# First projections in rounds of 2, 4, 4, 4, 2 row chunks, the first norm's sum of squares on TensorE, the first round modulated chunk by chunk

## The chip, the cores and the metric

One core of a Trainium2 chip runs the whole block; the other cores are idle. The metric is the device time of one execution in microseconds. Before the change it is 1664.97 us, the median of three runs (1662.68, 1664.97 and 1665.35).

## What is computed

One transformer block on 256 tokens of 2048 channels, in float32. The part that the change touches is the beginning, up to the first projection:

```python
mod = einsum('bd,de->be', silu(c), w_ada) + b_ada       # 12288 columns: six vectors of 2048
sh1, sc1, gt1, sh2, sc2, gt2 = split(mod, 6)
h = rms_norm(x, norm1_g) * (1 + sc1) + sh1              # x * rsqrt(mean(x*x) + 1e-6) * g
proj = einsum('btd,dc->btc', h, w_in)                   # [256, 2048] x [2048, 10064]
...
x = x + gt1 * (mixed @ w_out)
h = rms_norm(x, norm2_g) * (1 + sc2) + sh2
x = x + gt2 * (square(relu(h @ w_up)) @ w_down)
```

Between proj and mixed stand a linear recurrence over the tokens with a decay (rwkv, 16 heads of 64) and an attention with compressed, selected and window keys (nsa, 16 heads), joined by gates that are columns of proj as well.

## The kernel before, in words

**Layout.** Activations are kept transposed: a chunk is 128 channels on the partitions by 256 tokens, and 16 chunks make the 2048 channels. A projection multiplies weight tiles (two chunks, that is 256 rows of the weight matrix, by 512 columns, 0.5 MB; the tile of the first group has 352 columns) with h. Every float32 operand is split into two float32r parts, hi and lo, and each product is three matmuls: hi with hi, hi with lo, lo with hi (`mm3`, line 101). A weight tile goes through `weights` (line 217): a load by SP into one of four `raw` buffers, the hi part by ScalarE (`split`, line 189), the lo part by VectorE (line 191), each into one of three buffers. A tile of four column blocks gives 2 x 4 x 3 = 24 matmuls of 128 x 128 by 256 columns, the tile of the first group 18.

**Modulation columns.** The vector mod is made 128 columns at a time on VectorE: a dot of a [128, 2048] tile of w_ada transposed (1 MB) with silu(c), which stands on all partitions (`ada_long`, line 165, `ada_dot`, line 156). `modc[:, e]` is column block e; h of chunk j wants blocks j (shift) and 16 + j (scale), so two dots a chunk and 32 for all. The four tiles of the first round have a buffer each; all later ones take turns in two (`SLOTS = 2`, lines 163 to 171). From the rounds' end on, the other 64 column blocks come by half tiles through the `raw` buffers (`ada`, line 173).

**Norm 1** (lines 280 to 309). ScalarE squares two chunks at a time, VectorE adds the eight squares up in `sqs`, and two float32 matmuls with ones sum them over the channels into `pss`. `rs` is 1 / sqrt of it (`rsqrt`, line 297): logarithm and exponential on ScalarE and four small VectorE instructions.

**The start in rounds** (lines 182 and 379 to 396). The first projections have nine groups of columns: the small one (three tiles of up to 128 columns, to `pl`), keys of rwkv (two groups, to `prk`), values (two, which stay in PSUM, `pvp`), receptance (two, `prk`) and nsa queries (two, `pq`). Since h is not complete at first, they go by rounds over the rows:

```python
rounds = [(0, 2), (2, 2), (4, 4), (8, 4), (12, 4)]      # first chunk, number of chunks
```

A round with n chunks makes `am` (one small VectorE instruction for all n) and the n chunks of h (`modulate`, line 321, and `affine`, line 314: VectorE makes `hf`, ScalarE `hhi`, VectorE `hlo`), and then passes over all nine groups with the n/2 weight tiles of each. At the end of a group in a round its PSUM banks are copied out by ScalarE (first round) or added to what is there by VectorE (later rounds), 14 banks in a round (`acc_evac`, line 349). While a round goes on, the dots that the next one wants are spread over its weight tiles, by `pace` (line 388): as many dots for each tile as makes them all due one tile before the round's end. In the last round the two groups of queries are not run at once but put into `queue`.

**What sets the order.** The program is written in one order, and a planner with its own costs orders each engine's instructions at compile time: by priority, and among those that are ready by its reckoning. The start has the first priority, then the stream of weights and modulation (`prio(STREAM)`), then the rest. On the chip every engine goes through its own fixed order, and SP, which issues the loads, does too: an instruction that waits holds up those behind it on its engine.

**After the start.** The recurrence and the attention are chains of small instructions; between them `fill(n)` (line 264) takes steps of the projections in `queue`, half a weight tile each (12 matmuls): the queries of the last round, keys, values and merge gates, later the output projections of the branches. What is left of the queue is run at line 1067. Then come w_out, norm 2, up and down, all by the same weight stream.

Of the kernel before, what the change touches and what calls it, by code (L numbers as in the profile page):

```python
# [17 lines left out]
T = 256  # L18
# [6 lines left out]
# columns of the packed per-channel parameters  # L25
P_BADA, P_N1, P_N2, P_MU, P_A0, P_KK, P_KA, P_RK, P_LNW, P_LNB = 0, 96, 112, 128, 155, 163, 171, 179, 187, 195
P_QG, P_KG0, P_KG1, P_KG2, P_PEK, P_PEV, NPRM = 203, 204, 205, 206, 207, 223, 239
# columns of the packed constants
# [4 lines left out]
def block_kernel(ctx, tc, a):  # L33
# [116 lines left out]
    hold = []       # what the stream's next vector instructions have to stay behind  # L150
# [14 lines left out]
    def ada_long(e):  # L165
        """The same as ada, by one long load."""
        n = apn[0] if apn[0] < 4 else apn[0] % SLOTS
        r = apb[n // 2][:, n % 2]
        apn[0] += 1
        nc.sync.dma_start(r, a["w_ada_t"][e * 128:(e + 1) * 128])  # L170
        ada_dot(r, sb, prm[:, P_BADA + e:P_BADA + e + 1], modc[:, e:e + 1])

    def ada(e):
        """modc[:, e] = b_ada + w_ada[:, e*128:(e+1)*128]^T silu(c)"""
        part = sm.tile([128, 1], FT, name="adap", tag="sm1")
        for h in range(2):
            r = RAW("ar", [128, 1024])
            nc.sync.dma_start(r, a["w_ada_t"][e * 128:(e + 1) * 128, h * 1024:(h + 1) * 1024])
            ada_dot(r, sb[:, h * 1024:(h + 1) * 1024], part if h else prm[:, P_BADA + e:P_BADA + e + 1],
                    modc[:, e:e + 1] if h else part)  # L180

    rounds = [(0, 2), (2, 2), (4, 4), (8, 4), (12, 4)]
# [10 lines left out]
    # ones of head blocks and of chunk suffixes  # L193
# [6 lines left out]
    def head_sums(ps, jp, x):  # L200
        """Rows 32 jp and 32 jp + 1 of ps: the sums over the channels of the two heads of a tile of x."""
        mm(ps[32 * jp:32 * jp + 32], cs[:, C_HS:C_HS + 32], x)

    def spread(ps, jp, r):
        """These rows of r, given in two parts, on the 64 channels of either head."""
        for k in range(2):
            mm(ps, sel[32 * jp:32 * jp + 2], r[k][32 * jp:32 * jp + 2], k == 0, k == 1)
# [9 lines left out]
    def weights(segs, W):  # L217
        """segs: (source [256 rows, w], column, w); the two parts of [128, 2, W]."""
        with prio(STREAM):
            r = RAW("wr", [128, 2, W])  # L220
            for src, c0, w in segs:
                lastw[0] = nc.sync.dma_start(r[:, :, c0:c0 + w], src.rearrange("(k p) c -> p k c", p=128)).ins
            hi = whip.tile([128, 2, W], FR, name="whi", tag="whi")
            lo = wlop.tile([128, 2, W], FR, name="wlo", tag="wlo")
            split(r, hi, lo)
        return hi, lo

    starting = [True]
    later = []      # modulation columns still to come,
    pace = [0, 0]   # so many for each weight tile, and what has added up  # L230
# [8 lines left out]
    def proj(segs_of, W, ms, rhi, rlo, kps, evac, banks=None, first=True, last=True):  # L239
        """Transposed projection: out[m] [128, 256] = w[:, m]^T h over the chunk pairs kps; a generator  # L240
        that stops after every half of a pair; the last pair goes by banks."""
        nb = (len(ms) + 1) // 2
        ps = banks or [PM("pp") for _ in range(nb)]
        for i, kp in enumerate(kps):
            hi, lo = weights(segs_of(kp), W)
            next_ada(ada_long if starting[0] else ada)
            todo = [[(k, m) for m in range(len(ms))] for k in range(2)]
            if 0 and i == len(kps) - 1 and nb == 2:
                todo = [[(k, m) for k in range(2) for m in range(len(ms)) if m // 2 == b] for b in range(2)]
            for part in todo:  # L250
                for k, m in part:
                    (c0, cw), kc = ms[m], 2 * kp + k
                    o = ps[m // 2][0:cw, (m % 2) * 256:(m % 2) * 256 + 256]
                    mm3(o, hi[:, k, c0:c0 + cw], lo[:, k, c0:c0 + cw], rhi[:, kc], rlo[:, kc],
                        first and i == 0 and k == 0 and m % 2 == 0, last and i == len(kps) - 1 and k == 1)
                yield
        if evac:
            with prio(STREAM):
                for b in range(nb):
                    evac(b, ps[b])  # L260
# [3 lines left out]
    def fill(n=1):  # L264
        """The next n steps of the projections that nothing waits for yet."""
# [14 lines left out]
    pss = PX("pss", (128, 256))  # L280
    sqs = T2("sqs", [128, 2, T])
    act(sqs, xn[:, 0:2], AF.Square)
    for i in range(1, 8):
        sq = T2("sq", [128, 2, T])
        act(sq, xn[:, 2 * i:2 * i + 2], AF.Square)
        tt(sqs, sqs, sq, OP.add)
    for k in range(2):
        mm(pss, ones, sqs[:, k], k == 0, k == 1)

    def log_exp(behind):  # L290
        """The table set with both functions, behind these instructions."""
# [5 lines left out]
    def rsqrt(out, x, scale, ep, tmp):  # L297
        """out = 1 / sqrt(x * scale + ep): by logarithm and exponential, then one Newton step."""
# [15 lines left out]
    def affine(t, x, scale, r, shift, hi, lo, last=[None]):  # L314
        """The two parts of x * scale * r + shift."""
# [5 lines left out]
    def modulate(j0, n, src):  # L321
        """h chunks j0..j0+n from the normed ones."""
        last = [None]
        for j in range(j0, j0 + n, 2):
            hf = T2("hf", [128, 2, T])
            for i in range(2):
# [34 lines left out]
    # (columns, width, tiles, destination of a bank; None: stays in PSUM)  # L361
# [17 lines left out]
    for r, (j0, n) in enumerate(rounds):  # L379
        first, last = r == 0, r == len(rounds) - 1  # L380
        with prio(START + (1 << 18)):
            stt(am[:, j0:j0 + n], modc[:, 16 + j0:16 + j0 + n], 1.0, prm[:, P_N1 + j0:P_N1 + j0 + n], OP.add, OP.mult)
            lasth = modulate(j0, n, xn)
# [60 lines left out]
    def shift_mix(p, col, rows=slice(0, 128)):  # L444
        """p + (shifted p - p) mu for one channel tile [rows, 256]."""
# [5 lines left out]
    # lora inputs  # L451
# [18 lines left out]
    # the branches' gates of nsa  # L470
# [8 lines left out]
    # 1 + tanh(z / 2) in token rows; its suffix sums over chunks of 32 tokens give the decays  # L479
# [37 lines left out]
    # k: normed keys, learning rates  # L517
# [58 lines left out]
    # rows (chunk parity, b | k, token), columns a | r tokens  # L576
# [15 lines left out]
    # inverses of (I - L): one 32 x 32 system per head and chunk, by columns  # L592
# [34 lines left out]
    # token rows of v, b, k  # L627
# [11 lines left out]
    # what enters u without a state: (a k^T) v  # L639
# [27 lines left out]
    # ---- nsa: queries. They are kept in reverse order inside blocks of 128 tokens, so that the  # L667
    # bias of query p and key s depends on p + s -------------------------------------------
# [128 lines left out]
    # keys normed and on both halves of the partitions; [token, (selected | window), d] values  # L797
# [83 lines left out]
    # ---- nsa: compressed keys and values  # L881
# [46 lines left out]
    # rows (four head pairs, head, block), columns (half of the pairs, head, channel)  # L928
# [94 lines left out]
    # y_b, added with its gate; its first half keeps up with the heads  # L1023
# [41 lines left out]
    # ---- y_b, the rest  # L1065
# [61 lines left out]
    # the residual and gt2 by tokens  # L1127
# [69 lines left out]
def _pack(inp):  # L1197
    """Layout only: what the kernel reads, under the names that it reads it by."""
# [45 lines left out]
```

## Time and profile before

| | |
|---|---|
| median of three runs | 1664.97 us (1662.68 to 1665.35) |
| profiled execution, first to last instruction | 1663.5 us |
| TensorE busy | 1595.8 us, 96% |
| TensorE weight loads busy | 1459.8 us, 88% |
| VectorE busy | 1132.9 us, 68% |
| ScalarE busy | 754.1 us, 45% |
| bytes moved | 382 MB, mean 230 GB/s |

The page gives the span of the profiled execution and no time of its own around it; the three timed runs lie from 0.8 us below to 1.9 us above that span. Matmuls overlap in their pipeline, so that the duration of one (0.28 us) is more than the distance to the next (0.12 us). The share of an engine is a mean over stages with different limits; the start, which the change touches, is the first 243 us. A releaser named in a row is the instruction whose signal came last, which need not be the one that was slow.

### The profile page before, as it was taken

What the parts mean: (1) busy time and instruction counts of PE and PEld (TensorE: products, weight loads), DVE (VectorE), ACT (ScalarE), POOL (GpSimd) and SP (SyncE); (2) the same over time, 40 slices, a digit from 0 to 9 for tenths busy, and PEclk for the clock granted to TensorE, in tenths of its full rate; (3) what the DMA queues carried; (4) which work ended last, traced back from release to release, by engine and by line L of the source; (5) the groups of instructions that cost most, each with busy time, mean ns of one, the idle gap of its engine ahead of it and who ended that gap; (6) DMA issues with size and microseconds to landing.
All of it is one profiled execution on the core that took longest, in us unless ns stands there. A gap on an engine that the chain in (4) does not pass through costs nothing.

```text
span 1663.5 us, 30084 instructions
## 1 busy us (share of the span) xinstructions
PE 1595.8 (96%) x12310; PEld 1459.8 (88%) x12310; DVE 1132.9 (68%) x1632; ACT 754.1 (45%) x1079; POOL 35.6 (2%) x60
## 2 busy tenths in 40 slices
PE   5969999999999999999999899999999999999998
PEld 3968998889899889777999899999999888888886
DVE  7999876977778667777866766665654555555555
ACT  4423458527323275655534544444444444444442
POOL 0000000000000000000000000000000000000001
PEclk9989999997999999999999999999999999999999
DMA  9999767674878677654787477777776655665664
GB/s 364 318 333 346 241 192 233 207 219 153 276 220 273 224 260 264 230 169 156 266 286 258 153 239 246 247 235 252 237 203 182 204 196 190 195 196 190 193 193 147
DMA packets 171197, 382.11 MB, mean 230 GB/s; under 512 B 29281, under 2 KB 43921, under 8 KB 166706
## 3 DMA queue, kind: packets, MB, share of 16 engines
q1 hardware_dynamic: 149344, 355.79, 65.3%
q0 software_dynamic: 4192, 14.17, 2.4%
q10 hardware_dynamic: 17523, 10.24, 2.1%
q8 instruction: 96, 1.57, 0.4%
q14 instruction: 42, 0.34, 0.1%
HBM read 370.13 MB, written 10.01 MB: 229 GB/s over the span
## 4 chain that ended last, share of the span: by engine, by line
PE 76%; DVE 10%; DMA 8%; ACT 3%; issue 3%; ACTq 0%; DVEq 0%; SPq 0%
PE pp L99 45%; PE da L99 10%; PE db L99 10%; DVE wlo L90 3%; DMA ar<-in_w_ada_t 2%; DMA wr<-in_w_out 2%; PE pvp L99 2%; DVE ap L158 2%; PE y L99 1%; ACT whi L189 1%; PE po L99 1%; PE zps L99 1%; PE ups L99 1%; DMA kx<-skv 1%; DMA wr<-in_w_up 1%
## 5 line engine op out<-in xcount | busy, mean ns | idle before, releaser
L189 ACT CAST whi<-wr 128x1024 fp32r<-128x1024 f32 (+1 forms) x352 | 366.6, 1042 | 509.1 <-PE pp L99 305.6
L90 DVE TENSOR_TENSOR wlo<-wr,whi 128x1024 fp32r<-128x1024 f32 (+1 forms) x352 | 426.0, 1214 | 215.9 <-ACT whi L189 215.0
L99 PE MATMUL pp<-hhi,whi 128*128 128x256 f32 (+1 forms) x1072 | 309.8, 292 | 21.8 <-ACT hhi L87 20.8
L99 PE MATMUL pp<-hhi,wlo 128*128 128x256 f32 (+1 forms) x1072 | 302.2, 290 | 6.2 <-DVE wlo L90 6.2
L99 PE MATMUL pp<-hlo,whi 128*128 128x256 f32 (+1 forms) x1072 | 307.3, 289 | 0.2 <-DVE hlo L93 0.2
L99 PE MATMUL pp<-h2h,wlo 128*128 128x256 f32 x1024 | 289.0, 283 | 0.5 <-DVE wlo L90 0.5
L99 PE MATMUL pp<-h2l,whi 128*128 128x256 f32 x1024 | 289.0, 283 | 0.2 <-DVE h2l L93 0.2
L99 PE MATMUL pp<-h2h,whi 128*128 128x256 f32 x1024 | 287.2, 283 | 1.0 <-ACT h2h L87 1.0
L90 DVE TENSOR_TENSOR wdl<-wd,wdh 128x1024 fp32r<-128x1024 f32 x128 | 156.7, 1225 | 170.3 <-ACT wdh L189 170.0
L99 PEld LDWEIGHTS pp<-hhi,whi 128*128 128x128 f32 (+1 forms) x1072 | 209.2, 196 | 30.7 <-ACT hhi L87 22.1
L189 ACT CAST wdh<-wd 128x1024 fp32r<-128x1024 f32 x128 | 134.9, 1055 | 195.8 <-PE db L99 192.1
L99 PEld LDWEIGHTS pp<-hhi,wlo 128*128 128x128 f32 (+1 forms) x1072 | 206.1, 196 | 13.0 <-DVE wlo L90 8.5
L99 PEld LDWEIGHTS pp<-hlo,whi 128*128 128x128 f32 (+1 forms) x1072 | 209.9, 196 | 3.9 <-issue 2.7
L99 PEld LDWEIGHTS pp<-h2h,wlo 128*128 128x128 f32 x1024 | 196.4, 192 | 0.8 <-DVE wlo L90 0.7
L99 PEld LDWEIGHTS pp<-h2l,whi 128*128 128x128 f32 x1024 | 196.5, 192 | 0.6 <-DVE h2l L93 0.6
L99 PEld LDWEIGHTS pp<-h2h,whi 128*128 128x128 f32 x1024 | 195.4, 192 | 1.3 <-ACT h2h L87 1.3
L158 DVE CUSTOM_DVE_ANT_0 ar<-ar,sb,prm 128x1024 f32<-128x1024 f32 x64 | 82.0, 1281 | 53.8 <-DMA ar<-in_w_ada_t 53.8
L158 DVE CUSTOM_DVE_ANT_0 ar<-ar,sb,adap 128x1024 f32<-128x1024 f32 x64 | 81.9, 1280 | 15.4 <-DMA ar<-in_w_ada_t 15.0
L99 PE MATMUL da<-wdh,uh 128*128 128x512 f32 x256 | 78.9, 389 | 1.0 <-ACT uh L189 1.0
L99 PE MATMUL db<-wdl,uh 128*128 128x512 f32 x256 | 79.5, 389 | 0.0
L99 PE MATMUL db<-wdh,uh 128*128 128x512 f32 x256 | 79.2, 389 | 0.0
L99 PE MATMUL da<-wdh,ul 128*128 128x512 f32 x256 | 79.1, 389 | 0.0
(331 smaller groups left out, 2566.4 us busy)
## 6 DMA issues: line engine op xcount, KB each, us to landing
wr<-in_w_in SPq DMA_DIRECT2D x136, 512.0 KB, 5.0
ar<-in_w_ada_t SPq DMA_DIRECT2D x128, 512.0 KB, 4.4
wr<-in_w_up SPq DMA_DIRECT2D x128, 512.0 KB, 4.2
wd<-in_w_down SPq DMA_DIRECT2D x128, 512.0 KB, 4.3
ap<-in_w_ada_t SPq DMA_DIRECT2D x32, 1024.0 KB, 6.7
wr<-in_w_out SPq DMA_DIRECT2D x32, 512.0 KB, 5.5
wr<-in_w_in SPq DMA_DIRECT2D x40, 256.0 KB, 3.5
wr<-in_w_o_rwkv SPq DMA_DIRECT2D x16, 512.0 KB, 4.8
```

The lines of the kernel that those rows point to most:

```text
L90: return V.tensor_tensor(out, x, y, op=op).ins
L99: PE.matmul(out, l, r, start=start, stop=stop, skip_group_check=True)
L158: V.tensor_tensor_reduce(out=r, in0=r, in1=s, scale=0.5, scalar=start, op0=OP.mult, op1=OP.add, accum_out=out)
L189: S.copy(hi, raw)
```

## The change

Three edits, in code that otherwise stays as it is (the diff also takes out comments and docstrings, which is left out here). The rounds have 2, 4, 4, 4 and 2 chunks in place of 2, 2, 4, 4 and 4. The squares of norm 1 are not added up on VectorE: every one goes to TensorE, whose matmuls with ones add all 16 halves up in the PSUM bank. In the first round `am` is made for one chunk at a time, each directly before that chunk is modulated, into an `hf` tile of its own.

```diff
-    rounds = [(0, 2), (2, 2), (4, 4), (8, 4), (12, 4)]
+    rounds = [(0, 2), (2, 4), (6, 4), (10, 4), (14, 2)]
...
     pss = PX("pss", (128, 256))
-    sqs = T2("sqs", [128, 2, T])
-    act(sqs, xn[:, 0:2], AF.Square)
-    for i in range(1, 8):
+    for i in range(8):
         sq = T2("sq", [128, 2, T])
         act(sq, xn[:, 2 * i:2 * i + 2], AF.Square)
-        tt(sqs, sqs, sq, OP.add)
-    for k in range(2):
-        mm(pss, ones, sqs[:, k], k == 0, k == 1)
+        for k in range(2):
+            mm(pss, ones, sq[:, k], i == 0 and k == 0, i == 7 and k == 1)
...
         for j in range(j0, j0 + n, 2):
             hf = T2("hf", [128, 2, T])
-            for i in range(2):
+            for i in range(min(2, n)):
                 affine(hf[:, i], src[:, j + i], am[:, j + i:j + i + 1], rs, modc[:, j + i:j + i + 1], hhi[:, j + i], hlo[:, j + i], last)
...
         with prio(START + (1 << 18)):
-            stt(am[:, j0:j0 + n], modc[:, 16 + j0:16 + j0 + n], 1.0, prm[:, P_N1 + j0:P_N1 + j0 + n], OP.add, OP.mult)
-            lasth = modulate(j0, n, xn)
+            step = 1 if first else n
+            for j in range(j0, j0 + n, step):
+                stt(am[:, j:j + step], modc[:, 16 + j:16 + j + step], 1.0, prm[:, P_N1 + j:P_N1 + j + step], OP.add, OP.mult)
+                lasth = modulate(j, step, xn)
```

## Rows read from the trace of the kernel before

**Rows 1.** The page: its first line, and the busy time, share of the span and instructions of TensorE and VectorE.

```profile
span 1663.5 us, 30084 instructions
PE 1595.8 (96%) x12310; PEld 1459.8 (88%) x12310; DVE 1132.9 (68%) x1632; ACT 754.1 (45%) x1079; POOL 35.6 (2%) x60
```

**Rows 2.** Busy time of the engines in stretches: the five rounds, then the rest in three pieces. Columns: stretch, its length, busy us (and instructions) of each engine, granted TensorE clock, DMA share, GB/s.

```profile
28.40:56.60 28.20, 27.95 (x211) 27.66 (x212) 23.27 (x26) 15.38 (x25) 0.00 (x0) 1.00 0.93 336
56.60:94.70 38.10, 25.74 (x212) 25.23 (x210) 36.80 (x43) 10.99 (x14) 0.00 (x0) 0.88 0.95 324
94.70:148.00 53.30, 50.98 (x400) 50.08 (x400) 50.91 (x60) 20.25 (x25) 0.00 (x0) 0.96 0.94 344
148.00:204.00 56.00, 53.34 (x442) 53.09 (x443) 49.58 (x59) 19.94 (x23) 0.00 (x0) 1.00 0.82 276
204.00:243.00 39.00, 39.00 (x327) 38.83 (x325) 28.65 (x40) 22.48 (x32) 0.00 (x0) 1.00 0.63 182
243.00:800.00 557.00, 545.98 (x5102) 481.79 (x5101) 415.99 (x823) 283.67 (x540) 20.20 (x38) 0.96 0.69 222
800.00:950.00 150.00, 139.81 (x1124) 136.71 (x1123) 111.95 (x155) 67.41 (x83) 8.37 (x13) 0.99 0.72 241
950.00:1660.00 710.00, 703.74 (x4493) 642.78 (x4492) 393.95 (x394) 299.99 (x323) 6.79 (x6) 1.00 0.66 209
```

**Rows 3.** What TensorE waited for between 20 and 100 us (first line) and between 100 and 205 us (the others): us in total, times, the longest.

```profile
PE pp L99 <- ACT hhi L87: 20.8, 2, 11.7
...
PE pp L99 <- DVE wlo L90: 3.7, 3, 2.2
PE pvp L99 <- ACT whi L189: 1.0, 1, 1.0
```

**Rows 4.** TensorE's matmuls in order of time: the first of the projections, the last of round 1, the first of round 2. Columns: start us, us, what, with the idle time before it and who ended that.

```profile
28.48 1.22 PE L99 MATMUL pp<-hhi,whi 128*128 128x256 f32 x4 [9.15 <-ACT hhi L87]
...
82.82 0.28 PE L99 MATMUL pp<-hhi,wlo 128*128 128x256 f32 x1
94.77 1.22 PE L99 MATMUL pp<-hhi,whi 128*128 128x256 f32 x4 [11.67 <-ACT hhi L87]
```

**Rows 5.** VectorE in order of time: hlo of round 0, the first dot behind it, the first dot for round 2, the end of the eighth, am and hf of round 2. Columns as in rows 4.

```profile
29.34 0.87 DVE L93 SCALAR_TENSOR_TENSOR hlo<-hf,modc,hhi 128x256 fp32r<-128x256 f32 x2
30.13 2.34 DVE L158 CUSTOM_DVE_ANT_0 ap<-ap,sb,prm 128x2048 f32<-128x2048 f32 x1
...
53.86 2.35 DVE L158 CUSTOM_DVE_ANT_0 ap<-ap,sb,prm 128x2048 f32<-128x2048 f32 x1
...
93.38 0.08 DVE L158 DVE_READ_ACCUMULATOR2_ANT modc<- 128x1 f32 x1
93.49 0.16 DVE L93 SCALAR_TENSOR_TENSOR am<-modc,prm 128x4 f32<-128x4 f32 x1
93.69 1.67 DVE L93 SCALAR_TENSOR_TENSOR hf<-xn,am,rs 128x256 f32<-128x256 f32 x4
```

**Rows 6.** Pieces of the chain that ended last: start us, us, what. The first matmuls of round 2, a long run of matmuls in round 3 and 4, and the first work of the recurrence on TensorE.

```profile
94.77 15.21 PE pp L99 x108
...
181.45 38.36 PE pp L99 x320
...
242.84 0.25 PE gnp L475 x2
```

**Rows 7.** The granted clock in a stretch of the wait before round 2: stretch, length, TensorE busy, clock, DMA share, GB/s.

```profile
86.00:88.00 2.00, 0.00 (x0) 0.50 0.73 219
```

**Rows 8.** The loads: the first 20 us of the rows by stretch (columns as in rows 2), the next 8 us (columns as in rows 7), and the time from issue to landing of the modulation tiles between 28 and 100 us.

```profile
0.00:20.00 20.00, 9.24 (x12) 3.66 (x12) 13.43 (x27) 10.27 (x17) 0.20 (x4) 1.00 0.92 349
...
20.00:28.00 8.00, 0.00 (x0) 1.00 1.07 415
...
DMA to landing us min/median/max: 4.9/6.3/7.1
```

**Rows 9.** VectorE's groups of instructions: the splits in round 0 (28.4 to 56.6 us), and the adds of partial sums in round 1 (56.6 to 94.7 us). Columns: what xcount, busy us, mean ns, idle time before and what ended it.

```profile
L90 DVE TENSOR_TENSOR wlo<-wr,whi 128x1024 fp32r<-128x1024 f32 (+1 forms) x9 | 10.6, 1185 | 4.9 <-ACT whi L189 4.9
...
L90 DVE TENSOR_TENSOR prk<-prk,pp 128x512 f32<-128x512 f32 x8 | 5.3, 679 | 0.0
L90 DVE TENSOR_TENSOR pq<-pq,pp 128x512 f32<-128x512 f32 x4 | 2.6, 682 | 0.0
L90 DVE TENSOR_TENSOR pl<-pl,pp 128x512 f32<-128x512 f32 (+1 forms) x2 | 1.1, 549 | 1.2 <-PE pp L99 1.2
```

**Rows 10.** The first 22 us in order of time: TensorE's start matmuls (cps) with two of their weight loads, the last add of the squares on VectorE, the sum over the channels on TensorE, and the first of rsqrt's VectorE instructions.

```profile
2.74 7.16 PE L99 MATMUL cps<-crow,one 1*128 1x512 f32 x8 [2.74 <-DMA crow<-in_c]
...
4.58 0.33 PEld L99 LDWEIGHTS cps<-crow,one 1*128 1x128 f32 x1 [0.52 <-issue]
5.43 0.33 PEld L99 LDWEIGHTS cps<-crow,one 1*128 1x128 f32 x1 [0.52 <-issue]
...
16.52 0.69 DVE L90 TENSOR_TENSOR sqs<-sqs,sq 128x512 f32<-128x512 f32 x1
17.26 2.08 PE L99 MATMUL pss<-sqs,cs 128*128 128x256 f32 x4 [7.36 <-DVE sqs L90]
...
21.67 0.42 DVE L90 TENSOR_TENSOR rst<-rs 128x256 f32<-128x256 f32 x1
```

## The prediction

> **What bounds the kernel now.** I read the page's engine rows first [rows 1]: TensorE is busy for 1595.8 of 1663.5 us, VectorE for 1132.9. So an edit is worth what it takes out of the 68 us in which TensorE has nothing to do, wherever these lie. The stretches cut at the rounds come next [rows 2]: round 1 (56.6 to 94.7 us) holds 25.7 us of matmuls in 38.1 us, while VectorE is busy for 36.8 us of it; the rounds at 94.7 and 148 lose 2.3 and 2.7 us; from 204 to 243 us TensorE never stops, and from 243 us to the end it idles 28 us in 1417. The list of TensorE's waits [rows 3] puts 20.8 us on two waits for hhi, the longer one of 11.7 us, 3.7 us on wlo and 1.0 us on whi. The matmuls in order of time [rows 4] place them: 9.2 us of idling before the first projection at 28.48, and 11.67 us between 83.1 and 94.77, at the start of round 2. Last, VectorE in order of time [rows 5] says why: the eight modulation dots for round 2 begin at 53.86, the eighth ends at 93.46, and only then come am (93.49) and hf (93.69). The wait is for the eighth dot, not for ScalarE, which the list names.
>
> A full-speed matmul costs 0.120 us (320 in 38.36 us, [rows 6]). A round of two chunks has nine weight tiles, 18 + 8 x 24 = 210 matmuls, 25.2 us; one of four chunks 50.4 us. The 108 matmuls behind 94.77 take 15.21 us where 12.96 would do: 2.2 us more go to the clock, which stands at 0.50 of full speed (1.2 GHz) from 86 us, 3 us into the idling [rows 6, 7].
>
> **The change, part by part.** *Rounds 2, 4, 4, 4, 2.* Matmuls, weights, dots and the adds of partial sums stay in number (five rounds either way). What moves is how many dots must be done at each border: 12, 20, 28, 32 of the 32, behind 25, 76, 126 and 176 us of matmuls, where it was 8, 16, 24, 32 behind 25, 50, 101 and 151. So the long wait before the third round goes, and the border behind round 0 is late next: its pace becomes 8/(9-1), one dot for each weight tile, as in round 1 of before.
>
> Call T1 the time at which that second round starts its matmuls. Behind it stands what stands behind 94.77 in before: rounds of four with eight dots each, from the same state, plus 25.2 us, since 14 chunks are left and not 12. So the end moves by T1 + 25.2 - 94.77 = T1 - 69.6. [...]
>
> T1 from four sides:
> - Bytes. 349 GB/s for 20 us and 415 for 8.4 [rows 8] make 10.5 MB by 28.4 us. Wanted before the last dot: xT 2.1, constants 0.5, 12 modulation loads of 1.05, nine weight tiles 4.55, a tile or two of the next round 0.4 to 0.9: 20.3 MB. The other 9.8 MB at round 0's 336 GB/s [rows 2] take 29.2 us: 57.6. With the dot (2.4) and am, hf, hhi (93.46 to 94.77 in before, 1.3): 61.3.
> - VectorE, if it never idles: at 28.2 it still has one wlo and two hlo (2.0), 8 dots with their reads (8 x 2.35 = 18.8), 6 wlo of 1.16 (7.0) and up to three of the next round (3.0) [rows 5, 9]: 59.0, with 1.3 it is 60.3. Its 4.9 us of idling in round 0 [rows 9] are the room that four of the dots fill.
> - The two slots for long loads: the pair of dots from 30.13 ends at 34.75 (2 x 2.31), as now; then three turns of issue to landing 6.3 [rows 8], dot 2.4, issue 0.3: 34.75 + 27.0 + 1.3 = 63.1.
> - The cadence of round 1: eight dots in 39.6 us (53.86 to 93.46). In round 0 the partial sums are copied by ScalarE, so the 14 adds (5.3 + 2.6 + 1.1 = 9.0 us, [rows 9]) are not between them: 30.13 + 30.6 + 1.3 = 62.0.
>
> I take 62.0, the one that rests on the same mix of loads, dots and splits; ends 60.3 and 63.1. TensorE is through with round 0 at 56.6, so it waits some 5 us there in place of 11.7 later, and 14 chunks follow: **62.0 - 69.6 = -7.6 us**.
>
> The next two borders I cost at nothing: they are rounds 2 and 3 of before, whose 53.3 and 56.0 us [rows 2] stay. The round behind them has four dots: 50.9 - 4 x 2.35 = 41.5 us of VectorE work under 50.4 us of matmuls, so it hides; ends 0 and +2 (a wait as the 3.7 us of [rows 3] halved). The last round leaves four steps of 12 matmuls for the filler queue in place of eight: the recurrence begins about 2 us earlier and 5.8 us of matmuls have moved ahead of it. The filler behind it still holds 32 steps of keys, 16 of values and 128 of merge gates, and TensorE is busy for 546 of 557 us there [rows 2], so 0; ends -1 and +5.8 (all four steps missed).
>
> *Norm 1.* Seven adds of 0.69 leave VectorE. Six stand in its idle time before 14.25; the one at 16.52 is inside the unbroken row of dots [rows 10]: -0.6. TensorE gets 32 instructions for four. The start matmuls, 512 columns, follow each other every 0.86 us (7.2 us for eight with the tail, [rows 10]), so 256 columns cost 0.43: 13.8 us. They queue behind the start matmuls, which end at 9.9, so pss is done at 23.7, not 19.4, and nothing else stands behind them until 28.48. VectorE's first rst moves from 21.67 to 24.7 at the earliest. VectorE waits there if that order stays (+3.0); it loses nothing if splits and the next dots are put ahead. With the 0.6, ends of -0.6 and +2.4 on T1. I take 0, since three wlo (3.2 us) and two landed dots are at hand.
>
> The page "TensorE: Matmul & The Clock Gate" of the Trainium skill (Part 1: The HAM clock gate) says that sustained activity releases the throttle. By it the sums would run at full speed after their first part, and pss would be ready near 19.4 again. This case speaks against taking that for granted: eight back-to-back matmuls of one row kept 0.86 us a piece to the end.
>
> *First round chunk by chunk.* One more am (0.16 us for four columns, [rows 5]); hf and hlo of chunk 0 go ahead of chunk 1's dots if rs is there. TensorE could start some 1.5 us earlier, or 1 us later with the late rs; it waits before T1 anyway, so 0, ends -0.6 and +0.5 on T1.
>
> **Sum**: -7.6 on a profiled execution of span 1663.5. The runs shown have a median 1.5 us above it; the same step from the median gives 1657.4.
>
> **The rivals.**
> (a) *No wait at the second round.* At 415 GB/s [rows 8] the 9.8 MB land by 52.0, and only VectorE is left: T1 of 60.3 less the prefetched splits (3.0), 57.3. Then -12.3, and if so short a wait leaves the clock up, 2.2 more: 1650.5 to 1652.7. For it: early stretches held that rate; against: no stretch with both kinds of load did [rows 2]. The Trainium skill, "Perfetto Trace Analysis" (Roofline), puts the ceiling of one core's 16 DMA engines at about 435 GB/s; by that the bytes would be in at 50.9.
> (b) *The other side: two slots pace the dots.* If round 0 repeats round 1's cadence whole (39.6 us for eight dots), because loads wait for slots and weight loads wait behind them in SP's queue, T1 = 30.13 + 39.6 + 1.3 = 71.0, +1.4: 1666.4. It decides from T1 = 69.6. For it: one load to one tile, the same mix; against: VectorE idled for only 1.2 us in round 1, it was full, and 9.0 us of that were adds that round 0 has not [rows 9].
> (c) *Given back.* rs late with VectorE waiting in its order (+2.4), a wait in the four-dot round (+2), or filler steps missed (up to 5.8): -5 to 0, about 1660 to 1665. For it: both orders are fixed by the planner's own costs. Against: each has work to hide it.
>
> **How the numbers follow.** Forecast 0.58, its own range 1654 to 1661 (T1 58.6 to 65.2, the four sides and the norm's ends); (a) 0.12; (b) 0.08; (c) 0.22. About 0.2%, 3.3 us, is what a measurement can tell here, so faster is T1 under 66.3 with nothing given back: 0.58 + 0.12 + half of (c), 0.81, taken down to 0.79; slower is part of (b), 0.07; the rest, 0.14, is no change. The range reaches into (a) and over nearly all of (c): 1651.5 to 1664.
>
> **What would show it.** Right: the 11.7 us wait for hhi gone; one of 3 to 8 us near 57 to 62; VectorE without idle time from 30 us to it, and the copies of round 0 on ScalarE; rounds of 53 and 56 us behind it; the first rwkv work (242.84 in before, [rows 6]) near 240. pss matmuls from 6 to 24 us in 32 instructions. Wrong: T1 past 66; a second wait of several us at the next borders; TensorE idling over 28 us from 243 us on; VectorE idle near 22 us.

## The result: slower, and the profile after

The changed kernel takes 1679.18 us (median of six runs, 1672.9 to 1684.37) against 1663.83 us (six runs, 1660.03 to 1667.75): a ratio of 1.0088, 95% interval 1.0067 to 1.011. The forecast was 1657.4 us, the range 1651.5 to 1664. Six more runs, taken with the experiments, have a median of 1675.84 us and a ratio of 1.0078 (1.0059 to 1.0097). The execution that was profiled first took 1673.09 us (1.8 us more than its span), one of the two shortest; a second one, of 1681.45 us, is used beside it below. A ratio here is taken against runs of the kernel before that were made alongside (their medians: 1664.08 us for experiments 1 to 4, 1665.57 for 5 to 7, 1663.84 for 8 and 9) and is not quite the quotient of the medians. One of the six runs of experiment 4, of 1951.43 us at a granted clock of 0.74, was a slow one and is not counted in its median.

The page of the first, the two lines that answer to [rows 1]:

```profile
span 1671.3 us, 30135 instructions
PE 1601.5 (96%) x12338; PEld 1465.3 (88%) x12338; DVE 1127.5 (67%) x1626; ACT 755.8 (45%) x1079; POOL 35.5 (2%) x60
```

TensorE is busy 5.7 us more. The squares alone take 6.9 us more (9.0 us where it was 2.1), in time that was idle before, so without them it is busy 1.2 us less: the loss is time in which TensorE is idle. The stretches, cut at round 0, at the wait behind it, and then at the points where the h of a round is made, which is about when the round begins on VectorE's side (columns as in [rows 2]):

```profile
27.10:54.50 27.40, 27.13 (x210) 26.63 (x210) 22.89 (x22) 14.39 (x23) 0.00 (x0) 0.93 0.99 368
54.50:66.38 11.88, 0.00 (x1) 0.01 (x1) 8.77 (x11) 2.10 (x4) 0.00 (x0) 0.65 1.00 365
66.38:103.50 37.12, 35.84 (x273) 35.33 (x274) 36.42 (x40) 12.62 (x14) 0.00 (x0) 0.93 0.92 335
103.50:149.50 46.00, 42.82 (x339) 42.02 (x338) 44.91 (x54) 16.45 (x19) 0.00 (x0) 0.96 0.97 360
149.50:173.40 23.90, 23.52 (x193) 23.05 (x192) 23.90 (x31) 10.26 (x13) 0.00 (x0) 1.00 0.81 275
173.40:247.90 74.50, 74.50 (x623) 74.40 (x621) 53.85 (x71) 35.33 (x45) 0.00 (x0) 1.00 0.66 192
247.90:800.00 552.10, 533.23 (x5039) 469.76 (x5038) 410.17 (x816) 281.61 (x536) 20.15 (x37) 0.97 0.69 221
```

Three things are to be seen. TensorE stands still for 11.9 us behind round 0: the 11.67 us of [rows 4] did not go, they moved. From 173.4 us to the recurrence it never stops, as in before. And behind the recurrence's start it idles for 18.9 us up to 800 us, where it was 11.0 [rows 2].

TensorE's matmuls in order of time: the last of round 0, the first of the second round, and the first work of the recurrence (they answer to [rows 4, 6]):

```profile
54.20 0.28 PE L99 MATMUL pp<-hhi,wlo 128*128 128x256 f32 x1
...
66.38 1.22 PE L99 MATMUL pp<-hhi,whi 128*128 128x256 f32 x4 [11.89 <-ACT hhi L87]
...
247.94 0.32 PE L474 MATMUL gnp<-cs,gt 48*128 48x48 f32 x2
```

So T1, the start of the second round, is 66.4 and not 62.0, and the recurrence begins 5.1 us later than in before (242.84), where "near 240" was forecast. What holds T1 up is read on VectorE in order of time, from the first dot for the second round to am (compare [rows 5]):

```profile
28.83 2.35 DVE L158 CUSTOM_DVE_ANT_0 ap<-ap,sb,prm 128x2048 f32<-128x2048 f32 x1
...
31.10 2.35 DVE L158 CUSTOM_DVE_ANT_0 ap<-ap,sb,prm 128x2048 f32<-128x2048 f32 x1
...
34.25 1.23 DVE L90 TENSOR_TENSOR wlo<-wr,whi 128x1024 fp32r<-128x1024 f32 x1 [0.80 <-ACT whi L189]
35.95 1.23 DVE L90 TENSOR_TENSOR wlo<-wr,whi 128x1024 fp32r<-128x1024 f32 x1 [0.47 <-ACT whi L189]
38.68 1.23 DVE L90 TENSOR_TENSOR wlo<-wr,whi 128x1024 fp32r<-128x1024 f32 x1 [1.51 <-ACT whi L189]
39.83 2.35 DVE L158 CUSTOM_DVE_ANT_0 ap<-ap,sb,prm 128x2048 f32<-128x2048 f32 x1
...
43.23 2.35 DVE L158 CUSTOM_DVE_ANT_0 ap<-ap,sb,prm 128x2048 f32<-128x2048 f32 x1
...
50.27 2.35 DVE L158 CUSTOM_DVE_ANT_0 ap<-ap,sb,prm 128x2048 f32<-128x2048 f32 x1
...
53.75 2.35 DVE L158 CUSTOM_DVE_ANT_0 ap<-ap,sb,prm 128x2048 f32<-128x2048 f32 x1
...
58.81 2.35 DVE L158 CUSTOM_DVE_ANT_0 ap<-ap,sb,prm 128x2048 f32<-128x2048 f32 x1 [1.50 <-DMA ap<-in_w_ada_t]
...
62.70 2.35 DVE L158 CUSTOM_DVE_ANT_0 ap<-ap,sb,prm 128x2048 f32<-128x2048 f32 x1 [1.53 <-DMA ap<-in_w_ada_t]
...
65.10 0.16 DVE L93 SCALAR_TENSOR_TENSOR am<-modc,prm 128x4 f32<-128x4 f32 x1
```

Two slots hold loads for dots, and a slot is filled again only when its dot is done: SP issues the loads of the third, fourth and fifth dot right behind the first, second and third.

```profile
31.21 0.34 SPq L170 DMA_DIRECT2D ap<-in_w_ada_t  x1
...
33.48 0.34 SPq L170 DMA_DIRECT2D ap<-in_w_ada_t  x1
...
42.21 0.34 SPq L170 DMA_DIRECT2D ap<-in_w_ada_t  x1
```

The third dot waits in VectorE's order behind three splits, each of which stands idle until ScalarE has cast its tile (0.80, 0.47, 1.51 us). ScalarE in turn has waited for TensorE: 5.15 us before the copies at 32.69, behind which it casts the first two of these tiles, and 0.72 us before the cast at 37.60. Such a load lands after 4.7 to 6.5 us (median 5.7, 28 to 66 us), so those issued at 31.21 and 33.48 are in by 37.7 and 40.0; they are used at 39.83 and 43.23. From the end of one dot in the second slot to the end of the next it takes 12.1, 10.5 and 9.0 us (33.37, 45.5, 56.0, 65.05). The last two dots wait for their loads. VectorE's idle time by group, 28 to 66.3 us (columns as in [rows 9]):

```profile
L158 DVE CUSTOM_DVE_ANT_0 ap<-ap,sb,prm 128x2048 f32<-128x2048 f32 x8 | 18.7, 2347 | 3.0 <-DMA ap<-in_w_ada_t 3.0
L90 DVE TENSOR_TENSOR wlo<-wr,whi 128x1024 fp32r<-128x1024 f32 (+1 forms) x10 | 11.6, 1158 | 4.5 <-ACT whi L189 4.4
```

The 4.9 us that the splits idled in round 0 of before are still there (4.5), with twice the dots beside them.

### The profile page after: what moved, and what is told of

It is laid out like the page before. It is cut to its first block, busy times and chain, and to the rows that moved or that the text cites. A ratio compares the mean times of both kernels' runs of the same rounds, so it can differ in the third digit from the quotient of the medians.

```text
span 1671.3 us, 30135 instructions
## 1 busy us (share of the span) xinstructions
PE 1601.5 (96%) x12338; PEld 1465.3 (88%) x12338; DVE 1127.5 (67%) x1626; ACT 755.8 (45%) x1079; POOL 35.5 (2%) x60
## 4 chain that ended last, share of the span: by engine, by line
PE 76%; DMA 10%; DVE 8%; ACT 3%; issue 3%; ACTq 0%; DVEq 0%; SPq 0%
PE pp L99 44%; PE da L99 10%; PE db L99 10%; DMA ar<-in_w_ada_t 4%; DVE wlo L90 3%; PE pvp L99 2%; DMA ap<-in_w_ada_t 2%; DMA wr<-in_w_out 1%; DVE ap L158 1%; DMA wr<-in_w_up 1%; ACT whi L189 1%; PE ups L99 1%; PE po L99 1%; DVE ar L158 1%; PE zps L99 1%
## 5 line engine op out<-in xcount | busy, mean ns | idle before, releaser
L99 PE MATMUL pp<-hhi,whi 128*128 128x256 f32 x1072 | 308.9, 292 | 26.0 <-ACT hhi L87 20.2
L99 PE MATMUL pp<-hlo,whi 128*128 128x256 f32 x1072 | 307.9, 289 | 0.2 <-DVE hlo L93 0.2
L99 PEld LDWEIGHTS pp<-hhi,whi 128*128 128x128 f32 x1072 | 209.2, 196 | 29.7 <-ACT hhi L87 20.8
L99 PEld LDWEIGHTS pp<-hlo,whi 128*128 128x128 f32 x1072 | 209.7, 196 | 5.8 <-issue 4.6
L99 PE MATMUL da<-wdl,uh 128*128 128x512 f32 x256 | 79.1, 389 | 0.0
```

The source lines that it names most:

```text
L99: PE.matmul(out, l, r, start=start, stop=stop, skip_group_check=True)
```

## The experiments

Two theories came out of the traces for a loss where a gain was forecast. **R**: the end hangs on the recurrence; four of the eight query steps now stand ahead of it and not in the filler queue, 48 matmuls or 5.8 us, and nothing behind repays them. **O**: the order on VectorE, splits ahead of dots, makes T1 late. Rivals: the norm or the modulation by chunks did it; the two slots did; the queue's length does not matter (**W**).

**1. The rounds alone, in the kernel before.**

```diff
-    rounds = [(0, 2), (2, 2), (4, 4), (8, 4), (12, 4)]
+    rounds = [(0, 2), (2, 4), (6, 4), (10, 4), (14, 2)]
```

> The kernel before with the rounds 2, 4, 4, 4, 2 alone; norm 1 and the first round as before. Theory G (the rounds win nothing at the start, since the wait moves from 94.8 to some 66 us, and behind 248 us TensorE loses 8 to 15 us because four filler steps fewer are left and the stream reaches the keys and values earlier): +10 to +16 us against before, the whole of the change's loss; wait for hhi at the second round of 9 to 12 us, ending near 66 to 67 us; TensorE idle 28 to 32 us between 200 and 960 us. Rival N (the squares on TensorE and the chunk-by-chunk round shift the planner's order and cost the most): within 5 us of before.

Measured: 1680.09 us, ratio 1.0116 (1.0092 to 1.014), 16 us more by the medians and 19 by the ratio. T1 is 69.44 behind a wait of 13.64 us, where 66 to 67 and 9 to 12 were expected, and the recurrence begins at 250.7; TensorE's idle time between 200 and 960 us is 34.3 us (21.4 in before, 32.1 in the change). The rounds hold the whole loss.

**2. The other two edits alone:** the changed kernel with the old line of rounds.

```diff
-    rounds = [(0, 2), (2, 4), (6, 4), (10, 4), (14, 2)]
+    rounds = [(0, 2), (2, 2), (4, 4), (8, 4), (12, 4)]
```

> The change without its rounds: 2, 2, 4, 4, 4 with the squares summed on TensorE and the first round chunk by chunk. Theory G: within 2 us of before, or up to 2 us faster (first projection at 27.2 instead of 28.5 us, the 11.7 us wait at 94 us stays); TensorE idle near 20 us between 200 and 960. Rival N: +8 us or more.

Measured: 1662.13 us, ratio 0.9999 (0.9981 to 1.0017). The first projection starts at 27.70 in place of 28.48, the wait before the third round's matmuls is 14.39 us in place of 11.67 and ends at 95.96. What the start gains is waited away at a later border; this rival falls.

**3. Eight steps left in the queue.** The changed kernel; the queries' last four chunks (weight tiles 6 and 7) go to the queue, tile 5 is done in the round ahead.

```diff
+            tiles = len(groups) * n // 2 - (2 if r == len(rounds) - 2 else 0)
+            pace[:] = [len(later) / (tiles - 1), 0]
...
+            kps = range(j0 // 2, (j0 + n) // 2)
+            if cols[0][0] >= 3360 and W == 512 and r >= len(rounds) - 2:
+                kps = range(6, 8) if last else range(5, 6)
```

> The change, with the query groups' last four chunks (not two) left to the filler queue: eight filler steps as before the change, round 3 has two weight tiles fewer. Theory G in its narrow form (the four missing steps are what costs): the recurrence begins near 242 us, TensorE's idle time between 200 and 960 falls from 30 to about 20 us and the time comes back to within 3 us of before (-10 to -15 us against the change). Rival P (the loss behind the start comes of the planner's other order and of where the stream stands, whatever the number of steps): within 5 us of the change.

Measured: 1668.62 us, ratio 1.0028 (1.0011 to 1.0045), though T1 is 69.72 here, 3.3 us later than in the change. The recurrence begins at 246.1 and not near 242. By the ratios 8 to 10 of the 13 to 15 us are back, so the number of steps matters; but not by the way that was expected. TensorE's idle time between 200 and 960 us, which was to fall to about 20, is 33.3 us (32.1 in the change). The recurrence begins only 1.9 us earlier than in the change, and the granted clock from 245 to 650 us is 0.98 in place of 0.96.

**4. Four slots for the dots' loads.**

```diff
-    SLOTS = 2
+    SLOTS = 4
```

> The change, with four slots for the long modulation loads instead of two. Theory S (the dots of round 0 wait for two slots: 1.5 us of VectorE idle before the seventh and the eighth each, landing 6 to 7 us behind the issue): the second round begins at 59 to 62 us instead of 66.4, and the time falls by about 5 us. Rival D (the DMA engines are full and VectorE too, more loads in flight only land later): second round at 65 to 67 us, time within 2 us of the change.

Measured: 1688.81 us (median of five), ratio 1.0148 (1.0123 to 1.0172). The eighth dot ends at 58.1, 7 us earlier, and the wait for hhi is gone. But now TensorE waits for splits. Its waits from 60 to 250 us, and that kernel's stretch from 62 to 150 us:

```profile
PE pp L99 <- DVE wlo L90: 17.2, 9, 3.5
PE pvp L99 <- DVE wlo L90: 3.9, 1, 3.9
```

```profile
62.00:150.00 88.00, 67.33 (x476) 65.19 (x476) 85.60 (x100) 25.55 (x33) 0.00 (x0) 0.89 0.87 320
```

Ten waits of up to 3.9 us, and a clock of 0.89 as well: the recurrence begins at 266.9. VectorE is busy for 85.6 of the 88 us and idles there for no load; the dots, whose loads are now in early, stand in pairs ahead of splits in its order (those at 71.97 and 74.24 ahead of the split at 76.52, for which TensorE waits 3.5 us). The slots do pace the dots, but in this order more of them makes the splits late; S is right on the dots and wrong on the time.

**5. Four steps in the queue, in the kernel before.** Of the last round's queries, tile 6 is run at once, tile 7 queued.

```diff
+            kps = range(j0 // 2, (j0 + n) // 2)
+            if last and cols[0][0] >= 3360 and W == 512:
+                run(proj(wseg(cols), W, ms, hhi, hlo, range(6, 7), acc_evac(dst, False, False)))
+                kps = range(7, 8)
```

> The kernel before, with its own rounds, but of the query groups' last four chunks only two are left to the filler queue; the other two run at once in the last round (their partial sums are added in four more VectorE instructions of 0.7 us). Theory R (from the first work of the recurrence to the end each of the six profiled kernels takes 1417 to 1426 us, whatever is left to the queue, so the time goes with the recurrence's start): that start moves from 242.8 to 248 or 249 us and the time by +5 to +9 us. Rival W (TensorE's work sets the end: four steps moved from the queue to the front change nothing): within 2 us of before.

Measured: 1671.56 us, ratio 1.0038 (1.0013 to 1.0062): 6.3 us (2.2 to 10.3) for 5.8 us of matmuls moved ahead of the recurrence, which begins at 249.4. W is out and R holds, with rounds, norm and modulation as before.

**6. Sixteen steps in the queue, in the kernel before.** The queries' last eight chunks are left to it.

```diff
+            tiles = len(groups) * n // 2 - (4 if r == len(rounds) - 2 else 0)
...
+            if cols[0][0] >= 3360 and W == 512 and r >= len(rounds) - 2:
+                if not last:
+                    continue
+                kps = range(4, 8)
```

> The kernel before, with its own rounds, and the query groups' last eight chunks (not four) left to the filler queue, 16 steps and not 8. Theory R: the recurrence begins 8 to 12 us earlier, near 231 to 235 us, and the time falls by 6 to 12 us, more than either kernel. Rival W: within 3 us of before, since TensorE has the same matmuls; or slower, if the round of chunks 8 to 11 now waits for its dots.

Measured: 1667.07 us, ratio 1.0014 (0.9995 to 1.0032). The recurrence begins at 234.5, 8.3 us earlier, and nothing is gained: here W is right and R wrong. (The profiled execution, of 1661.88 us, is the shortest of its twelve; even in it 4.8 of the 8.3 us are lost again between the recurrence's start and the end.) TensorE's waits for splits of the streamed weights from 245 to 420 us are longer than in before, where they are 1.7 us:

```profile
PE pp L99 <- DVE wlo L90: 7.8, 4, 4.9
```

Which filler steps these waits belong to was not followed up. R is one-sided in these two runs: steps taken out of the queue are lost, steps added to it are not won.

**7. Dots ahead of splits in round 0.** In the changed kernel, the splits of weight tiles 6, 7, 9 and 10 are ordered behind the third to sixth dot.

```diff
+    AFTER = {6: 3, 7: 4, 9: 5, 10: 6}
...
+            d = AFTER.get(tile_no[0])
+            with tc.issue_after(dots[3 + d]) if d else contextlib.nullcontext():
+                split(r, hi, lo)
```

> The change, with four splits of the stream put behind dots in VectorE's order (the 6th tile's behind the 3rd dot of round 0, the 7th's behind the 4th, the 9th's behind the 5th, the 10th's behind the 6th). Theory O (the dots' loads had landed, but the dots stood behind splits that wait for buffers which TensorE frees; that cost the two slots 4.6 us in their first two turns): the second round begins at 60 to 62.5 us and not at 66.4, and the time falls by 4 to 6 us against the change, to some 1674. Rival D (DMA engines bound): second round at 65 to 67 us and no gain.

Measured: 1668.77 us, ratio 1.0031 (1.0011 to 1.005), 10 us less than the change's first six runs and 7 less than the six of experiment 9, where 4 to 6 were expected. T1 is 63.82, between what O (60 to 62.5) and D (65 to 67) expected. VectorE in order of time, the third to seventh dot:

```profile
37.10 2.34 DVE L158 CUSTOM_DVE_ANT_0 ap<-ap,sb,prm 128x2048 f32<-128x2048 f32 x1
...
40.51 2.34 DVE L158 CUSTOM_DVE_ANT_0 ap<-ap,sb,prm 128x2048 f32<-128x2048 f32 x1
...
46.71 2.35 DVE L158 CUSTOM_DVE_ANT_0 ap<-ap,sb,prm 128x2048 f32<-128x2048 f32 x1 [1.51 <-DMA ap<-in_w_ada_t]
...
51.20 2.35 DVE L158 CUSTOM_DVE_ANT_0 ap<-ap,sb,prm 128x2048 f32<-128x2048 f32 x1 [0.99 <-DMA ap<-in_w_ada_t]
...
57.88 2.35 DVE L158 CUSTOM_DVE_ANT_0 ap<-ap,sb,prm 128x2048 f32<-128x2048 f32 x1
```

The third dot is 2.7 us earlier with two splits ahead of it in place of three, and the turns of the second slot now take 9.4, 10.7 and 8.9 us. O has the direction for T1 and not the whole size: 2.6 of the 4.4 us over the forecast are the order's. The recurrence begins 2.3 us earlier than in the change (245.6); why the time fell by more was not found.

**8. Both repairs together** (the edits of 3 and 7).

> The change with both repairs: the four splits of round 0 behind their dots, and eight filler steps of queries left to the queue. Start of the second round's matmuls 63.8 us as in the kernel with the splits behind the dots, recurrence 5.8 us earlier than there, 240. Theory 'two separate losses': each repair gains what it gained alone (10.4 and 10.5 us of 1679): 1658 to 1661, below the kernel before. Rival 'the chain's start counts only down to some point, as the version of before with sixteen steps showed': 1663 to 1667, no better than the better of the two alone by more than 5 us.

Measured: 1665.80 us, ratio 1.0018 (1.0004 to 1.0032). T1 is 64.85, the recurrence begins at 243.4 and not at 240. The rival has it: by the medians 3 us better than either repair, which the intervals don't tell apart, and still not faster than before.

**9. The changed kernel again.**

> The changed kernel unaltered, for a second profiled execution and more times: its six times run from 1673 to 1684 and the profiled one is among the two shortest. Theory 'the start is fixed, the spread lies behind it': the second round starts its matmuls at 66.4 and the recurrence at 248, each within 1 us; the median is 1676 to 1682; what a longer execution has more of lies behind 245 us, as waits of TensorE. Rival 'the start itself varies with the loads': the second round starts 2 us or more later or earlier than 66.4, and the recurrence with it.

Measured: 1675.84 us (1673.21 to 1681.45); its profiled execution has a span of 1679.7 us, T1 67.08 and the recurrence at 252.3. T1 kept to 0.7 us, but the way from there to the recurrence took 185.2 us and not 181.6; so the first theory is right on T1 and wrong on the recurrence: 4.4 of the 8.4 us between the two executions are there when it begins. TensorE's waits between 60 and 250 us in this execution, the first line being the wait before T1:

```profile
PE pp L99 <- ACT hhi L87: 12.1, 1, 12.1
PE pp L99 <- DVE wlo L90: 2.8, 4, 1.3
PE pp L99 <- ACT whi L189: 2.5, 2, 1.6
PE pp L99 <- DVE prk L90: 1.4, 2, 1.0
PE pvp L99 <- ACT whi L189: 1.2, 1, 1.2
```

All runs side by side. "Behind T1" is the time from T1 to the recurrence, less what the matmuls there need by the pace of before (148.07 us for its 12 chunks with eight steps queued, 25.2 for two chunks, 5.8 for four steps, 11.5 less for eight more steps queued; for the kernels with the old rounds T1 is the third round's start). "To the end" is the time from the recurrence's first matmul to the end of the profiled execution. "Idle" is the sum of TensorE's idle times of 0.2 us and more that end in a stretch, from 20 us to the recurrence's start and in the 740 us behind that.

| kernel | T1 | behind T1 | recurrence | to the end | idle ahead, behind | ratio |
|---|---|---|---|---|---|---|
| before | 94.77 | 0 | 242.8 | 1420.7 | 26.3, 21.0 | 1 |
| 2: norm and chunks | 95.96 | +0.3 | 244.3 | 1417.0 | 28.4, 22.8 | 0.9999 |
| 5: four steps | 95.74 | -0.2 | 249.4 | 1417.6 | 27.0, 29.1 | 1.0038 |
| 6: sixteen steps | 96.14 | +1.8 | 234.5 | 1425.5 | 27.9, 25.7 | 1.0014 |
| the change | 66.38 | +2.5 | 247.9 | 1423.4 | 24.9, 31.8 | 1.0088 |
| 9: the change again | 67.08 | +6.2 | 252.3 | 1427.4 | 28.1, 34.1 | 1.0078 |
| 1: rounds alone | 69.44 | +2.2 | 250.7 | 1426.2 | 27.1, 34.3 | 1.0116 |
| 3: eight steps | 69.72 | +3.1 | 246.1 | 1420.5 | 28.3, 32.8 | 1.0028 |
| 7: dots ahead | 63.82 | +2.7 | 245.6 | 1423.5 | 23.8, 32.9 | 1.0031 |
| 8: both repairs | 64.85 | +5.2 | 243.4 | 1426.8 | 25.3, 29.1 | 1.0018 |
| 4: four slots | none | | 266.9 | 1421.5 | 34.2, 29.7 | 1.0148 |

Ahead of the recurrence the idle time hardly differs (experiment 4 aside); behind it every kernel with other rounds or another queue has 5 to 13 us more than before. Not all of this shows in the time, since the granted clock there is higher in some (0.98 from 245 to 650 us in experiment 3, 0.95 in before), and TensorE's busy time with it smaller. Experiment 5 idles 8 us more behind the recurrence's start than before and yet is through 3.1 us sooner. From there to the end the executions differ by up to 10 us, by 4.0 between two of the same kernel, so that a single profile does not tell what a few us behind the recurrence come from.

## Why the prediction was wrong

**What bounds the kernel** was read rightly, and the 11.67 us wait was rightly put on the eighth dot. Rows 5 showed where it comes from, but not that it would follow the dots to the next border.

**T1, step "Its 4.9 us of idling in round 0 [rows 9] are the room that four of the dots fill": wrong.** The idle time belongs to instructions that stand ahead of the dots in a fixed order, and a dot behind them cannot use it. The side "two slots" had the right form and was mis-sized: 34.75 + 3 x 9.0 + 1.3 = 63.1 was forecast, 33.37 + 12.1 + 10.5 + 9.0 + 1.3 = 66.3 came. Only the last turn was the 6.3 + 2.4 + 0.3 us of the working; in the first two, loads that had landed waited for VectorE. Bytes (61.3) and VectorE (60.3) were no bound: the DMA engines were busy for 99 to 100% of the time up to T1, but in experiment 4 the eighth dot ended at 58.1. Taking the cadence's 62.0 below the slots' 63.1 was the wrong choice: a term made of waits in a chain can't be beaten by an average. In experiments 1 and 3, with T1 of 69.4 and 69.7, dots and splits stand in the same order on VectorE, but the seventh dot waits 3.2 and 2.7 us for its load, in place of 1.5; why these loads came later was not followed up.

**"So the end moves by T1 + 25.2 - 94.77 = T1 - 69.6": incomplete, and the dearest step.** It holds for the rounds, but the paragraph of the prediction that moves 5.8 us of queries ahead of the recurrence costs them at "so 0; ends -1 and +5.8". Experiment 5 measured +6.3 us (2.2 to 10.3) for that alone. (The values behind it are 8 filler steps with matmuls of twice the columns and not 16 steps; the work is the same.) From TensorE's 546 busy us of 557 I took the queue to be what fills that stretch; but in that experiment the end went with the recurrence, and TensorE idled more behind its start (29.1 us against 21.0). By experiment 6 the reverse does not hold: a start that was 8.3 us earlier won nothing. With the +5.8, T1 = 66.4 gives +2.6 us, and the point from which the change loses is T1 = 63.8, 0.7 us above the latest of the four sides.

**The next two borders "at nothing": wrong by 2.5 us, 6.2 in the second execution.** Their ends were 0 and +2. Idle time on the way from T1 to the recurrence is as in before (4.8 us against 4.9 behind 94.77). But TensorE is busy there for 176.7 us with 1422 matmuls, and was for 143.1 with 1165: 257 more at 0.120 are 30.8 us, 33.6 came. Some 2.0 of the 2.7 us are matmuls at the lower level of the clock (1.2 GHz): 1.4 behind a group of small waits that was followed by a fall of the clock (last section; in experiment 3 the same waits were not), and 0.6 at the restart, where the 108 matmuls behind T1 take 15.6 us in place of 15.0 from the first start to that of the next one. In the second execution the idle time is longer as well. VectorE is full in these rounds (36.4 of 37.1 us, 44.9 of 46.0, 23.9 of 23.9), so each of its splits and adds that comes late is seen by TensorE. **The round with four dots** was rightly costed: 0.4 us of idling, and none from 173.4 us on.

**Norm 1: the size was wrong, the worth of nothing right.** The sums were done at 18.9 and not at 23.7. The 0.43 us for 256 columns were scaled from start matmuls at half pace. Two stretches with the last of the start matmuls and the first squares, then one with later squares (columns as in [rows 2]):

```profile
9.00:11.00 2.00, 2.00 (x5) 0.90 (x4) 0.69 (x1) 2.00 (x6) 0.00 (x0) 1.00 1.12 437
11.00:13.00 2.00, 2.00 (x6) 1.63 (x5) 0.69 (x1) 1.97 (x4) 0.00 (x0) 1.00 1.00 416
...
15.00:17.00 2.00, 2.00 (x11) 1.77 (x10) 2.00 (x3) 0.00 (x0) 0.00 (x0) 1.00 0.98 414
```

Five or six instructions in 2 us at first, eleven later (0.43 us apart up to 13.5 us and 0.22 from 13.8 us on), and not for want of squares: six of the eight pairs were there by 11.1 us. So the 0.43 was right for the first quarter of the 32 and twice too much for the rest. The page "TensorE: Matmul & The Clock Gate" of the Trainium skill (Part 1: The HAM clock gate) says that sustained activity releases the throttle. The change of pace agrees with it, and the 19.4 that I worked out by it was right to half a microsecond; the argument that I set against it, from one-row matmuls, was not. The first projection came 1.3 us earlier; by experiment 2 that is worth nothing, since the next border waits for dots anyway. **Chunk by chunk** at 0 agrees with the same run, which holds both edits; neither was tried by itself.

**The rivals.** (a), no wait, did not happen. (b), the slots, was nearer to the mechanism than the forecast: two slots paced the dots, but to a T1 of 66.4 and not 71.0, and its point of decision, 69.6, lacked the queue's 5.8 us. (c) named the right losses, a wait in a later round and filler steps missed, and added them to a gain of 7.6 that was not there. The range failed for the same reason: it took T1's late end, the wait's +2 and the queue's +5.8 as alternatives. Together, with the T1 that was measured, they make -3.2 + 2.0 + 5.8 = +4.6 us and end at about 1670, against 1672.9 of the change's shortest execution.

**What stays open.** 5.1 us of delay at the recurrence in the first profile and 9.5 in the second, against 13 to 15 us by the ratios. The two profiles are 7.8 and 16.2 us longer than that of before, so 2.7 and 6.7 us are lost behind the recurrence's start. What is lost there is seen as idle time (10.8 and 13.1 us more than before); in the first profile 5.7 us of it, in place of 1.7, are waits of the values' matmuls (psv) for splits (248 to 985 us):

```profile
PE psv L99 <- DVE wlo L90: 5.7, 4, 2.3
```

But experiments 5 and 7 have such waits as well (5.3 and 7.0 us) at less than half of the loss. Why the order of before idles less behind the recurrence than that of every other queue tried, one with more steps included, was not settled.

## What to carry to other kernels

Measure a moved border at the start of the next chain, here at the first instruction of the recurrence (a later start cost time here, an earlier one won none), and count everything that the edit puts ahead of it, even work that only leaves a queue behind it. Idle time of an engine that runs in a fixed order is room only for what stands ahead of the instruction that idles; where loads take turns in a few slots, add up the turns with whatever stands between a landed load and its use. Bounds that can all come true at once are added, not set beside each other.

## What the runs showed of the hardware

The same idling of TensorE is followed by a fall of its clock in one execution and not in the next. In the change (first execution) three waits of 2.1 us in all have four matmuls between them; the stretch stands behind them (length, busy times, then clock, DMA share, GB/s):

```profile
114.22 0.36 PE L99 MATMUL pp<-hhi,whi 128*128 128x256 f32 x1 [1.02 <-DVE prk L90]
...
115.13 0.39 PE L99 MATMUL pp<-hhi,whi 128*128 128x256 f32 x1 [0.43 <-DVE prk L90]
...
116.26 0.58 PE L99 MATMUL pp<-hhi,wlo 128*128 128x256 f32 x1 [0.64 <-DVE wlo L90]
```

```profile
116.00:121.00 5.00, 4.74 (x28) 4.74 (x29) 5.00 (x6) 0.76 (x1) 0.00 (x0) 0.66 0.64 171
```

The clock is granted at 0.66 on the mean, and 28 matmuls take 4.74 us in place of 3.4 (28 x 0.120). The second execution of the change and experiment 1 show the same waits and a fall near 120 us. Experiment 3 has the same three waits, and the clock stays up:

```profile
118.24 0.35 PE L99 MATMUL pp<-hhi,whi 128*128 128x256 f32 x1 [1.02 <-DVE prk L90]
...
119.14 0.39 PE L99 MATMUL pp<-hhi,whi 128*128 128x256 f32 x1 [0.43 <-DVE prk L90]
...
120.27 0.38 PE L99 MATMUL pp<-hhi,wlo 128*128 128x256 f32 x1 [0.64 <-DVE wlo L90]
```

```profile
120.00:125.00 5.00, 4.73 (x39) 4.73 (x40) 5.00 (x6) 0.78 (x1) 0.00 (x0) 1.00 0.66 155
```

It is so with one longer wait, too. In before, a wait of 2.20 us leaves the clock at full speed:

```profile
158.14 0.39 PE L99 MATMUL pp<-hhi,wlo 128*128 128x256 f32 x1 [2.20 <-DVE wlo L90]
```

```profile
158.00:162.00 4.00, 3.86 (x32) 3.86 (x33) 4.00 (x6) 1.05 (x1) 0.00 (x0) 1.00 0.83 285
```

In experiment 6, a wait of 2.19 us for a split is followed by a fall:

```profile
159.94 0.39 PE L99 MATMUL pp<-hhi,wlo 128*128 128x256 f32 x1 [2.19 <-DVE wlo L90]
```

```profile
160.00:165.00 5.00, 5.00 (x29) 5.00 (x30) 5.00 (x5) 1.04 (x1) 0.00 (x0) 0.66 0.87 295
```

So a fall behind waits of this size costs some 1.4 or 1.5 us where it comes (28 and 29 matmuls in 4.74 and 5.00 us), and these rows do not tell beforehand where it will.

The clock column can mislead at the start: it reads 1.00 from 9 to 17 us, while the pace of the squares' matmuls doubled in between.
